# A written order for the loads, norms and projections that open the first layer

## The chip, the cores and the metric

The kernel runs on one core of one Trainium2 chip. The metric is the device time of one execution in microseconds (us). The kernel before takes 2577.58 us, the median of 3 runs (2576.38 to 2580.35). A core has five engines that run side by side, each taking its instructions in the order in which they were laid down: PE (TensorE, the matrix products), DVE (VectorE), ACT (ScalarE), POOL (GpSimd) and SP (SyncE, which here issues almost all DMAs).

## The reference, cut to what matters

Four layers in a row on 1024 tokens of width 1024: two of a first block (with 256 context tokens beside them), two of a second. Only the first layer is touched. It is:

```python
h_l = rmsnorm(x, norm_g[l]) * (1 + sc_l[:, None]) + sh_l[:, None]
h_c = rmsnorm(ctx, norm_g[l]) * (1 + sc_c) + sh_c
f_in, f_gate, q_a, kv_a, k_pe, m_gate = split_cols(h_lat @ w_in, EVEN_SPLITS)
kv = (rmsnorm(kv_a, kv_norm) @ w_kvb)
q = (rmsnorm(q_a, q_norm) @ w_qb)
y_l = concatenate([fourier_mix(f_in) * silu(f_gate), a_l * silu(m_gate)]) @ w_out
```

`sh`, `sc` (shift and scale) are products of `silu(c)` with `w_mod`. `k_pe` and a part of `q` are rotated by the rope tables before the attention `a_l`.

## The kernel before, in words

All activations are kept transposed: features on the 128 partitions, tokens along the row. Tokens come in three chunks, `CH`: c=0 and c=1 are 512 tokens each, c=2 is the context with 256. Every f32 product is made from three matmuls, because activations and weights are split into a high part (rounded) and a low part (the rest): high by high, low by high, high by low. `wblk_steps` (L168) loads a block of weights in pieces into one of two buffers of raw data (`wraw`), ACT makes the high part (L158) and POOL the low part (L166); the split blocks lie in a pool with two slots (`wp`, L103) unless another pool is named.

**Who sets the order.** The program is traced once, and a planner at compile time then lays down each engine's order from priorities (earlier traced goes first if it is ready by the planner's own clock) and allots buffers. `later` (L133) lowers the priority of what is traced in it. `in_order` (L141) takes the instructions that one engine got while the block was traced and fixes their order among themselves; instructions traced outside can still be placed between them. `issue_after` puts instructions behind a given one on its engine.

**`e1_start`** (L505) opens the layer. `START` (L92) is a list of steps: `v` loads the small vectors, `xN` loads chunk N of the input (8 tiles), adds up its squares (ACT squares, DVE adds for c=0 and c=1, POOL for c=2) and then makes its norm (`norm`, L550); with an `a` behind it the norm is left to a step `rN`. A norm is `rstd_bc` (L373): column sums on PE (L358), nine small DVE operations (`rsqrt`, L339), products on PE that spread the result over the partitions (L369), and an ACT copy. `lN` loads a quarter of `w_mod` into four buffers `mraw`, `mN` multiplies it by `silu(c)` (L441, L447) and gives shift and scale for two feature tiles; `wN` loads two of the four pieces of a weight block: w0 is the block of `kv_a`, w1 the first 256 columns of `f_in`. As soon as a quarter q and a chunk c are both there, `modulate(q, c)` writes the two tiles `ah` and `al` of the projections' input on DVE and ACT (L489 to L497). In this block the orders of SP and of DVE are fixed; PE's is the planner's.

**`e1`** (L616) then makes `kv_a` (four tiles for c=0 and c=1) and four blocks of `f_in`, k by k as the inputs arrive; then `kv_a` of the context; then the norm of `kv_a` (`rstd_bc` into `rkt` and `rkb`); then the rest of `f_in` (token blocks j=4 to 9 of the first 256 columns, then all ten of the next 288, the last 32 of which are `k_pe`, copied into `kp` by DVE, L670 and L671); then `kp` is transposed on PE (L679), rotated on DVE and stored; then the key and value projections. `k_evac` (L692) scales each key tile by `rkb`. `mod_rest` (L455) is traced under `later`: 32 loads of 512 KB and 56 DVE passes over them (L474) that make the shifts and scales of later use. The query part follows: `q_a` (by `proj`, L233, with weight blocks of 256 and 128 columns), its squares added up by POOL in `accq` (L389), its norm, and the product with `w_qb`, whose evacuation (L724) needs the norm. Last, `fill` (L746) yields the gate tiles (the SiLU branches), eight steps of three matmuls to a tile: some are laid down under `later`, until `PRE1` = 48 times 512 columns are reached (L782), the others are spread through the attention, whose PE order is written out (`attention`, L267).

Of the kernel before, what the change touches and what calls it, by code (L numbers as in the profile page):

```python
# [15 lines left out]
ALU = mybir.AluOpType  # L16
# [4 lines left out]
P = 128  # L21
T = 1024
TC = 256
TT = T + TC
EPS = 1e-6
MLA_SCALE = float(1.0 / np.sqrt(96.0))
CH = ((0, 512), (512, 1024), (1024, 1280))
# [15 lines left out]
class Kern:  # L43
# [47 lines left out]
    PRE1 = 48  # L91
    START = "v x0a l0 w0 r0 m0 w0 x1 x2 w1 m1 w1 m2 m3"  # L92
    WAYS = "xxxxdddd xxxxdddd xxxxxxxx".split()
# [27 lines left out]
    def stg(self, n=512):  # L121
        return self.t(self.gp_, [P, 512], tag="stg", bufs=4)[:, 0:n]
# [382 lines left out]
    def e1_start(self):  # L505
        V = self.nc.vector
# [27 lines left out]
        act, M, acc = Act(), {}, {}  # L534
# [21 lines left out]
        H, N = set(), []  # L556
        with self.in_order(mybir.EngineType.SP), self.in_order(mybir.EngineType.DVE):
            for what in self.START.split():
                i = int(what[1:2] or 0)
# [56 lines left out]
    def e1(self):  # L616
# [7 lines left out]
        act = self.e1_start()  # L624
        w_in, w_out = A["e_w_in"], A["e_w_out"]
        ALLC = (0, 2, 1)
        mv = self.open("modv", side="left")
        with self.later():
            self.mod_rest(mv)
# [22 lines left out]
        for j, o in enumerate(us):  # L652
            t = stg()
            nc.scalar.activation(out=t, in_=o, func=AF.Copy)
            self.dma(u_scr[j * 256:(j + 1) * 256, 0:256].rearrange("(e p) n -> p e n", p=P), t.rearrange("p (e n) -> p e n", e=2))
        self.proj(wk, ((0, P, 0), (P, P, 1)), act, (2,), ev)
        rkt = self.t(kvp, [P, 10], nm="rkt")
        rkb = self.t(kvp, [P, TT], nm="rkb")
        self.rstd_bc(rkb, acc, TT, 256.0, rkt)
        kp = self.t(kvp, [P, 10, 64], nm="kp")  # L660
        for b, n in ((0, 256), (1, 288)):
            w = self.wblk(w_in, b * 256, n, pool=kvp) if b else wu
            for j in (0, 1, 2, 3, 8, 9, 4, 5, 6, 7) if b else (4, 5, 6, 7, 8, 9):
                s = self.sps()[:, 0:n]
                self.dense_tok(s, w, 0, n, act, j)
                o = stg(256)
                nc.scalar.activation(out=o, in_=s[:, 0:256], func=AF.Copy)
                self.dma(u_scr[j * P:(j + 1) * P, b * 256:(b + 1) * 256], o)
                if b:
                    V.tensor_copy(kp[:, j, 0:32], s[:, 256:288])  # L670
                    V.tensor_copy(kp[:, j, 32:64].rearrange("p (a b) -> p a b", a=2), s[:, 256:288].rearrange("p (a b) -> p a b", a=2)[:, ::-1, :])  # L671
        for c, (a, b) in enumerate(CH):
            tab = self.t(kvp, [32, 2, 512], tag="kpe_tab", bufs=1)
            if c < 2:
                self.dma(tab, A["kpe_tab"][:, :, a:b])
            for e in range(2 if c < 2 else 1):
                s = self.sps()
                for j in range(a // P, b // P):
                    nc.tensor.transpose(s[0:32, j * P - a:j * P - a + P], kp[:, j, 32 * e:32 * e + 32], self.ident)  # L679
                if c == 2:  # L680
                    V.tensor_copy(kpe[:, a:b], s[0:32, 0:b - a])
                elif e == 0:
                    V.tensor_tensor(kpe[:, a:b], s[0:32], tab[:, 0], ALU.mult)
                else:
                    o = stg()[0:32]
                    V.tensor_tensor(o, s[0:32], tab[:, 1], ALU.mult)
                    V.tensor_tensor(kpe[:, a:b], kpe[:, a:b], o, ALU.add)
        self.dma(kpe_scr, kpe)
        w_kvb, w_qb = A["e_w_kvb"], A["e_w_qb"]
        w = self.wblk(w_kvb, 0, 512)  # L690

        def k_evac(i, c, ps):  # L692
# [3 lines left out]
            self.dma(k_scr[i * P:(i + 1) * P, a:b], o)  # L696
        self.proj(w, [(i * P, P, i) for i in range(4)], KV, ALLC, k_evac)
        w = self.wblk(w_kvb, 512, 512)
# [13 lines left out]
        Q = Act(3)  # L712
        ev = self.normed_split(qp, "q", Q, gq, acc, sm)
        w = self.wblk(w_in, 1056, 256)
        self.proj(w, ((0, P, 0), (P, P, 1)), act, ALLC, ev)
        w = self.wblk(w_in, 1312, 128)
        self.proj(w, ((0, P, 2),), act, ALLC, ev)
        rqb = acc
        self.rstd_bc(rqb, acc, TT, 384.0)

# [19 lines left out]
        gate, mix, todo = self.gate_evac(gate_scr, None, gs, 2), Act(), []  # L740

        def gates(w, i, c):
            for e in (0, 1):
                yield from self.dense_steps(w, e * P, act, c, self.FT, lambda ps: gate(i + e, c, ps))

        def fill():  # L746

            for i, c0 in ((0, 544), (2, 800)):
                w = self.wblk(w_in, c0, 256)
                for c in ALLC:  # L750
                    yield from gates(w, i, c)
            W = [(self.wblk(w_in, c0, 256), i) for i, c0 in ((4, 1696), (6, 1952))]
            for c in ALLC:
                for w, i in W:
                    yield from gates(w, i, c)
                todo.extend((k, c) for k in range(8))

# [21 lines left out]
        am_scr = dram("am_scr", [512, TT])  # L779
        f, before = fill(), 0  # L780
        with self.later():
# [1381 lines left out]
```

## Time and profile before

| | us |
|---|---|
| median of 3 runs | 2577.58 |
| lowest, highest | 2576.38, 2580.35 |
| the profiled execution | 2578.05 |
| its span (first to last instruction) | 2576.2 |
| PE busy | 2428.7 (94%) |
| DVE, ACT, POOL busy | 1681.6, 1126.9, 895.3 |
| mean granted TensorE clock | 0.976 of full speed |

A row of a wait gives the total, how often, and the longest. A row of a window gives its length, the busy time of PE, of PE's weight loads, of DVE, ACT and POOL (instructions in brackets), then the granted clock, the share of the DMA engines that was busy, and GB/s. A row in order of time gives start, length, engine, line, operation, what is written from what, the sizes, and how many instructions are merged.

All times in the rows are counted from the start of the span. An engine's idle time stands in square brackets behind the instruction that ended it, with what was waited for. Matmuls overlap in the records, so the pace is read from start to start. The granted clock is given as a share of full speed: 1.00 is 2.4 GHz, 0.50 is 1.2 GHz, and a figure between is a mix of the two over the stretch.

### The profile page before, as it was taken

To read this page: it belongs to the slowest core of one execution; us is meant where nothing else is said; L and a number is where in the kernel's file an instruction comes from. 1 tells how busy PE (TensorE), PEld (TensorE's weight loads), DVE (VectorE), ACT (ScalarE), POOL (GpSimd) and SP (SyncE) were. 2 spreads that over 40 slices of the span, in tenths; PEclk is the share of its full clock that TensorE was granted. 3 is DMA by queue.
4 is the path that set the end of the run, shared out by engine and by line. 5 is a ranking of instruction groups with operands and counts; after the bars stand their busy time and mean duration, and the time that the engine had idled before them with its cause. 6 is when DMAs were issued, how large, how long until landed. Compare 5 with 4: busy or idle time off the path is not lost. (4 is left out here: it accounts for less than half of the span.)

```text
span 2576.2 us, 36051 instructions
## 1 busy us (share of the span) xinstructions
PE 2428.7 (94%) x12814; PEld 1962.3 (76%) x12814; DVE 1681.6 (65%) x2983; ACT 1126.9 (44%) x2201; POOL 895.3 (35%) x750
## 2 busy tenths in 40 slices
PE   5999999999999989999898999999999999999998
PEld 3887777777678877666666779887877877799888
DVE  6785447788855548777776463557888576773455
ACT  4412226666653325655565333345656333513331
POOL 4204243354411152332322225146452343453231
PEclk7999999999999999999999999999999999999999
DMA  7475432132324231221313513233233332201433
GB/s 240 137 223 197 155 105 57 47 102 76 96 82 146 84 90 52 67 87 52 101 64 111 164 66 97 90 108 98 85 105 122 101 114 79 70 21 49 165 111 103
DMA packets 217092, 265.16 MB, mean 103 GB/s; under 512 B 42768, under 2 KB 142768, under 8 KB 216784
## 3 DMA queue, kind: packets, MB, share of 16 engines
q1 hardware_dynamic: 216192, 262.75, 32.7%
q8 instruction: 101, 1.65, 0.3%
q14 instruction: 79, 0.65, 0.1%
q10 hardware_dynamic: 720, 0.10, 0.0%
HBM read 188.60 MB, written 71.97 MB: 101 GB/s over the span
## 5 line engine op out<-in xcount | busy, mean ns | idle before, releaser
L166 POOL TENSOR_TENSOR wlo<-wraw,whi 128x512 fp32r<-128x512 f32 (+3 forms) x229 | 318.3, 1401 | 608.3 <-ACT whi L158 531.4
L166 DVE TENSOR_TENSOR pl<-pf,ph 128x512 fp32r<-128x512 f32 (+1 forms) x328 | 258.6, 789 | 79.1 <-ACT pf L953 39.8
L158 ACT ACTIVATE whi<-wraw 128x512 fp32r<-128x512 f32 (+3 forms) x261 | 154.3, 613 | 341.5 <-PE s L209 53.2
L209 PE MATMUL s<-ah,whi 128*128 128x512 f32 (+1 forms) x392 | 159.3, 406 | 12.2 <-DVE hf L1725 5.9
L209 PE MATMUL s<-al,whi 128*128 128x512 f32 (+1 forms) x392 | 158.0, 403 | 1.8 <-DVE al L492 1.4
L209 PE MATMUL s<-ah,wlo 128*128 128x512 f32 (+1 forms) x392 | 157.4, 402 | 0.0
L953 ACT ACTIVATE ph<-s 128x512 fp32r<-128x512 f32 (+1 forms) x176 | 101.5, 577 | 105.8 <-PE s L950 104.9
L915 DVE TENSOR_REDUCE mx<-p 128x1 f32<-128x512 f32 (+1 forms) x208 | 116.7, 574 | 34.5 <-PE p L914 33.5
L1250 ACT ACTIVATE ph<-s 128x512 fp32r<-128x512 f32 x152 | 90.8, 597 | 108.7 <-PE s L1242 58.4
L209 PE MATMUL g<-ah,whi 128*128 128x512 f32 (+1 forms) x312 | 122.5, 393 | 3.3 <-DVE mixg L382 3.3
L209 PE MATMUL f<-ah,whi 128*128 128x512 f32 x304 | 123.2, 405 | 1.3 <-DVE stg L1361 0.8
L209 PE MATMUL f<-ah,wlo 128*128 128x512 f32 x304 | 122.8, 404 | 0.0
L209 PE MATMUL f<-al,whi 128*128 128x512 f32 x304 | 122.8, 404 | 0.0
L209 PE MATMUL g<-ah,wlo 128*128 128x512 f32 (+1 forms) x312 | 121.7, 390 | 0.0
L209 PE MATMUL g<-al,whi 128*128 128x512 f32 (+1 forms) x312 | 121.5, 390 | 0.0
L1614 DVE TENSOR_TENSOR_SCAN scu<-scu,ones_col 128x128 f32<-128x128 f32 (+3 forms) x64 | 97.4, 1535 | 14.4 <-ACT scu L1610 11.6
L1210 DVE CUSTOM_DVE_ANT_0 p<-p,maskt 128x384 f32<-128x384 f32 (+1 forms) x128 | 67.4, 529 | 58.1 <-PE p L1209 58.1
L953 ACT ACTIVATE pf<-s 128x512 f32<-128x512 f32 (+1 forms) x176 | 100.8, 573 | 2.0 <-DVE pl L166 1.9
L209 PEld LDWEIGHTS s<-ah,whi 128*128 128x128 f32 x392 | 75.3, 192 | 34.2 <-DVE hf L1725 6.8
L474 DVE CUSTOM_DVE_ANT_0 wmj<-wmt,srow,c_b_mod 128x1024 bf16<-128x1024 f32 x56 | 77.0, 1376 | 29.0 <-DMA wmt<-in_w_modT 28.0
L209 PEld LDWEIGHTS s<-al,whi 128*128 128x128 f32 x392 | 75.4, 192 | 20.6 <-DVE al L492 2.1
L1250 ACT ACTIVATE pf<-s 128x512 f32<-128x512 f32 x152 | 90.1, 593 | 0.1
(775 smaller groups left out, 7568.9 us busy)
## 6 DMA issues: line engine op xcount, KB each, us to landing
wmt<-in_w_modT SPq DMA_DIRECT2D x32, 512.0 KB
wraw<-in_even_w_in SPq DMA_DIRECT2D x56, 256.0 KB
wraw<-in_odd_w_in SPq DMA_DIRECT2D x48, 256.0 KB
wraw<-in_o_w_in SPq DMA_DIRECT2D x40, 256.0 KB
xold<-x_scr SPq DMA_DIRECT2D x40, 256.0 KB
mraw<-in_w_mod SPq DMA_DIRECT2D x16, 512.0 KB
x_scr<-x SPq DMA_DIRECT2D x32, 256.0 KB
mixx<-m_scr SPq DMA_DIRECT2D x30, 256.0 KB
```

The source lines that it names most:

```text
L158: nc.scalar.activation(out=out, in_=in_, func=AF.Copy)
L166: return e.tensor_tensor(out, in_, hi.bitcast(F32), ALU.subtract)
L209: self.nc.tensor.matmul(out, ws[:, k, c:c + m], a[k][ch], start=first and i == j == 0, stop=last and i == len(ks) - 1 and j == 2)
L474: V.tensor_tensor_reduce(out=junk, in0=w, in1=s[:, i], scale=0.5, scalar=self.bm[l][:, m, i:i + 1], op0=ALU.mult, op1=ALU.add, accum_out=s ...
L915: V.reduce_max(mx[:, e, j:j + 1], d[:, 0:y - x], axis=AX)
L953: nc.scalar.activation(out=t, in_=s, func=AF.Exp, scale=MLA_SCALE)
L1210: V.tensor_tensor_reduce(out=d[:, 0:n], in0=d[:, 0:n], in1=self.mask[:, off:off + n], scale=1.0, scalar=-3.0e38, op0=ALU.add, op1=ALU.max, ...
L1250: nc.scalar.activation(out=t, in_=s, func=AF.Exp, scale=0.125)
L1614: V.tensor_tensor_scan(out=rev, data0=rev, data1=self.ones.to_broadcast([P, n]), initial=1.0, op0=ALU.mult, op1=ALU.mult)
```

## The change

Four parts. (1) `START` is put into another order, and PE's order in this block is fixed too. The second chunk's load is split from its norm, the second quarter of `w_mod` is loaded and multiplied before that norm, and the context comes last. `mod_rest` is put behind the start's DMAs. (2) After the start PE's order is fixed as: `f_in` j=8, 9; `kv_a` of the context; j=4, 5; the sums of the norm; j=6, 7; the spreading of the norm; then the 288 columns. (3) The transposes of `kp` become a generator of five turns, of which two are taken after each chunk of the key projection, in a fixed PE order. (4) In the query part two gate tiles of c=0 (16 steps of `fill`) stand between the projection and its norm, in a fixed PE order; the 128-column weights move to the query part's own pool `qp`; the steps count towards `PRE1`. The cut diff:

```diff
-    START = "v x0a l0 w0 r0 m0 w0 x1 x2 w1 m1 w1 m2 m3"
+    START = "v x0a l0 r0 w0 m0 x1a w1 l1 m1 r1 w0 w1 l2 m2 l3 m3 x2"
...
-        with self.in_order(mybir.EngineType.SP), self.in_order(mybir.EngineType.DVE):
+        with self.in_order(mybir.EngineType.SP), self.in_order(mybir.EngineType.DVE), self.in_order():
...
-        with self.later():
+        with self.later(), self.tc.issue_after(self.first_dmas):
             self.mod_rest(mv)
...
-        self.proj(wk, ((0, P, 0), (P, P, 1)), act, (2,), ev)
...
-        self.rstd_bc(rkb, acc, TT, 256.0, rkt)
...
-        for b, n in ((0, 256), (1, 288)):
-            w = self.wblk(w_in, b * 256, n, pool=kvp) if b else wu
-            for j in (0, 1, 2, 3, 8, 9, 4, 5, 6, 7) if b else (4, 5, 6, 7, 8, 9):
+        def u_proj(w, b, n, js):
+            for j in js:
...
+        with self.in_order():
+            u_proj(wu, 0, 256, (8, 9))
+            self.proj(wk, ((0, P, 0), (P, P, 1)), act, (2,), ev)
+            u_proj(wu, 0, 256, (4, 5))
+            self.rstd_cols(acc, TT // P, 256.0, rkt)
+            u_proj(wu, 0, 256, (6, 7))
+            self.bcast_cols(rkt, TT // P, rkb)
+            u_proj(self.wblk(w_in, 256, 288, pool=kvp), 1, 288, (0, 1, 2, 3, 8, 9, 4, 5, 6, 7))
...
+        turns = rotate_kpe()
...
-        self.proj(w, [(i * P, P, i) for i in range(4)], KV, ALLC, k_evac)
+        with self.in_order():
+            for c in ALLC:
+                self.proj(w, [(i * P, P, i) for i in range(4)], KV, (c,), k_evac)
+                next(turns)
+                next(turns, None)
+            for _ in turns:
+                pass
...
+        gate = self.gate_evac(gate_scr)
...
+        f, before = fill(), 0
         w = self.wblk(w_in, 1056, 256)
-        self.proj(w, ((0, P, 0), (P, P, 1)), act, ALLC, ev)
-        w = self.wblk(w_in, 1312, 128)
-        self.proj(w, ((0, P, 2),), act, ALLC, ev)
+        w2 = self.wblk(w_in, 1312, 128, pool=qp)
         rqb = acc
-        self.rstd_bc(rqb, acc, TT, 384.0)
+        with self.in_order():
+            self.proj(w, ((0, P, 0), (P, P, 1)), act, ALLC, ev)
+            self.proj(w2, ((0, P, 2),), act, ALLC, ev)
+            for _ in range(16):
+                before += next(f)
+            self.rstd_bc(rqb, acc, TT, 384.0)
...
-        f, before = fill(), 0
         with self.later():
             while before < self.PRE1 * 512:
                 before += next(f)
```

`rotate_kpe` holds the old loop over `CH` with a `yield` after each transposed group, and `gates` and `fill` are moved up unchanged.

## Rows read from the trace of the kernel before

**Rows 1.** Page, busy time of PE.
```profile
PE 2428.7 (94%) x12814; PEld 1962.3 (76%) x12814; DVE 1681.6 (65%) x2983; ACT 1126.9 (44%) x2201; POOL 895.3 (35%) x750
```

**Rows 2.** PE in order of time, first layer up to the 288 columns.
```profile
28.73 0.79 PE L209 MATMUL s<-ah,whi 128*128 128x512 f32 x1 [3.23 <-ACT ah L490]
...
97.65 0.28 PE L221 MATMUL g<-whi,ach 128*128 128x256 f32 x1
...
107.59 0.36 PE L221 MATMUL o<-whi,ah 128*128 128x256 f32 x1
...
110.51 0.28 PE L221 MATMUL p<-whi,ah 128*128 128x256 f32 x1
...
123.42 0.29 PE L221 MATMUL s<-whi,ah 128*128 128x288 f32 x1
```

**Rows 3.** Windows of 20 us in the start.
```profile
40.00:60.00 20.00, 17.07 (x80) 9.82 (x84) 14.88 (x20) 5.73 (x12) 15.07 (x13) 0.75 0.50 162
...
60.00:80.00 20.00, 18.78 (x90) 12.05 (x83) 14.69 (x36) 8.57 (x17) 0.00 (x0) 0.83 0.38 123
```

**Rows 4.** DVE in order of time, in the start.
```profile
32.88 5.45 DVE L389 TENSOR_TENSOR acc<-acc,sq 128x512 f32<-128x512 f32 x7
...
48.02 3.55 DVE L489 SCALAR_TENSOR_TENSOR mh_t<-x,mc,rb 128x512 f32<-128x512 f32 x2 [2.86 <-ACT rb L371]
...
65.47 0.75 DVE L489 SCALAR_TENSOR_TENSOR mh_t<-x,mc,rb 128x512 f32<-128x512 f32 x1
...
77.03 0.55 DVE L495 TENSOR_SCALAR mh_t<-x,mc,ms 128x512 f32<-128x512 f32 x1
...
77.49 0.68 DVE L166 TENSOR_TENSOR al<-mh_t,ah 128x512 fp32r<-128x512 f32 x1
...
89.19 0.49 DVE L492 SCALAR_TENSOR_TENSOR acl<-mh_t,ms,ach 128x256 fp32r<-128x256 f32 x1 [0.18 <-ACT ach L490]
```

**Rows 5.** SP's DMA issues in the start, in order of time.
```profile
25.00 4.92 SPq L128 DMA_DIRECT2D x<-in_ctxT  x7
...
32.91 1.96 SPq L128 DMA_DIRECT2D mraw<-in_w_mod  x4
...
89.74 0.73 SPq L128 DMA_DIRECT2D kpe_tab<-in_kpe_tab  x1
```

**Rows 6.** DMA traffic in 40 slices of the first 100 us.
```profile
GB/s 60 297 296 256 377 403 240 2 132 323 325 376 339 231 321 352 117 123 309 0 51 278 264 155 256 356 349 20 0 0 7 0 0 0 0 0 115 283 358 168
```

**Rows 7.** DVE in order of time: the norm of `kv_a` and two passes.
```profile
116.60 0.16 DVE L360 TENSOR_SCALAR rs_s<-f 128x10 f32<-128x10 f32 x1
...
126.44 2.39 DVE L474 CUSTOM_DVE_ANT_0 wmj<-wmt,srow,c_b_mod 128x1024 bf16<-128x1024 f32 x1
...
131.41 0.17 DVE L351 SCALAR_TENSOR_TENSOR rkt<-rs_t,rkt 128x10 f32<-128x10 f32 x1
...
196.69 1.29 DVE L474 CUSTOM_DVE_ANT_0 wmj<-wmt,srow,c_b_mod 128x1024 bf16<-128x1024 f32 x1 [3.87 <-DMA wmt<-in_w_modT]
```

**Rows 8.** PE's waits from 94 to 400 us.
```profile
PE f L358 <- POOL accq L389: 4.6, 1, 4.6
...
PE f L369 <- DVE rkt L351: 3.1, 1, 3.1
...
PE g L679 <- DVE kp L670: 1.9, 1, 1.9
...
PE p L209 <- DVE kpe L683: 1.4, 1, 1.4
```

**Rows 9.** Windows behind two of these waits.
```profile
131.70:135.70 4.00, 3.97 (x19) 4.00 (x20) 2.78 (x7) 0.60 (x1) 0.00 (x0) 0.57 0.90 268
...
243.70:251.70 8.00, 7.96 (x26) 6.80 (x27) 8.00 (x9) 1.87 (x5) 6.17 (x6) 0.51 0.12 33
```

**Rows 10.** PE in order of time, ahead of the attention.
```profile
330.53 0.58 PE L209 MATMUL g<-ah,whi 128*128 128x512 f32 x1
...
352.91 0.40 PE L914 MATMUL p<-kh,qh 96*128 96x512 f32 x1
```

More of the change, by code (lines that the diff above doesn't have):

```diff
@@ L671, in e1 @@
                     V.tensor_copy(kp[:, j, 32:64].rearrange("p (a b) -> p a b", a=2), s[:, 256:288].rearrange("p (a b) -> p a b", a=2)[:, ::-1, :])
[L672 to L687, printed above, removed]
@@ L688, in e1, with rotate_kpe @@
-        self.dma(kpe_scr, kpe)
+        def rotate_kpe():
+            for c, (a, b) in enumerate(CH):
+                tab = self.t(kvp, [32, 2, 512], tag="kpe_tab", bufs=1)
+                if c < 2:
+                    self.dma(tab, A["kpe_tab"][:, :, a:b])
+                for e in range(2 if c < 2 else 1):
+                    s = self.sps()
+                    for j in range(a // P, b // P):
+                        nc.tensor.transpose(s[0:32, j * P - a:j * P - a + P], kp[:, j, 32 * e:32 * e + 32], self.ident)
+                    if c == 2:
+                        V.tensor_copy(kpe[:, a:b], s[0:32, 0:b - a])
+                    elif e == 0:
+                        V.tensor_tensor(kpe[:, a:b], s[0:32], tab[:, 0], ALU.mult)
+                    else:
+                        o = stg()[0:32]
+                        V.tensor_tensor(o, s[0:32], tab[:, 1], ALU.mult)
+                        V.tensor_tensor(kpe[:, a:b], kpe[:, a:b], o, ALU.add)
+                    yield
+            self.dma(kpe_scr, kpe)
@@ L713, in e1, with gates, fill @@
         ev = self.normed_split(qp, "q", Q, gq, acc, sm)
+        gate = self.gate_evac(gate_scr)
+        def gates(w, i, c):
+            for e in (0, 1):
+                yield from self.dense_steps(w, e * P, act, c, self.FT, lambda ps: gate(i + e, c, ps))
+        def fill():
+            for i, c0 in ((0, 544), (2, 800)):
+                w = self.wblk(w_in, c0, 256)
+                for c in ALLC:
+                    yield from gates(w, i, c)
+            W = [(self.wblk(w_in, c0, 256), i) for i, c0 in ((4, 1696), (6, 1952))]
+            for c in ALLC:
+                for w, i in W:
+                    yield from gates(w, i, c)
+                todo.extend((k, c) for k in range(8))
+        f, before = fill(), 0
         w = self.wblk(w_in, 1056, 256)
-        self.proj(w, ((0, P, 0), (P, P, 1)), act, ALLC, ev)
-        w = self.wblk(w_in, 1312, 128)
-        self.proj(w, ((0, P, 2),), act, ALLC, ev)
+        w2 = self.wblk(w_in, 1312, 128, pool=qp)
         rqb = acc
-        self.rstd_bc(rqb, acc, TT, 384.0)
+        with self.in_order():
[4 more added lines that the diff above has]
+            self.rstd_bc(rqb, acc, TT, 384.0)
         def q_evac(i, c, ps):
@@ L740, in e1 @@
         gate, mix, todo = self.gate_evac(gate_scr, None, gs, 2), Act(), []
[L742 to L756, printed above, removed]
         def add():
```

## The prediction, as it was made before the run

> **What bounds the kernel now.** I read the page's busy times first: PE is busy for 94% of the span [rows 1]. So time is to be had where PE stands still or runs at the lower clock, and I looked for these places in the stretch that the change touches, which ends with the first product of the attention at 352.9 us [rows 10]. The order of time on PE shows a first projection at 28.73 us and the last of that batch ending at 97.65, where block j=8 begins [rows 2]. The work between is about 48 us at full clock: 34.2 for the projections (four blocks of 24 products at 0.244 us and four at 0.122, twice and once the pace of 256 columns in rows 2: 110.51 - 107.59 = 2.92 us for 24), some 14 for shifts, scales and norms. 69 us passed. The windows say why: a granted clock of 0.75 and 0.83 of full speed [rows 3], PE being fed piece by piece.
>
> What feeds it is DVE, whose order is fixed. The order of time on DVE [rows 4]: the second chunk's squares are added until 38.3 us, its norm lets the first modulation of that chunk begin at 48.0, the context's last tile is written at 89.2, and only then does SP get past its release and issue the next loads at 89.74 [rows 5]. Call that moment E. The second quarter of `w_mod` is issued at 32.91, behind the context [rows 5], and the traffic has holes from 32.5 us on although 7 MB are still to come [rows 6]. After the start the list of PE's waits [rows 8] has four that matter: 4.6 us for the squares of `q_a` on POOL, 3.1 for the norm of `kv_a`, 1.9 and 1.4 around the transposes of `kp`. The windows behind the first two run at 0.51 and 0.57 of full clock [rows 9].
>
> **The change part by part.** Sums are made against the profiled execution, 2578.05 us (span 2576.2 and 1.85 around it), which lies 0.47 above the median.
>
> **The start.** Nothing is added or left out; 16 `mraw`, 24 input and 8 weight DMAs change places on SP, and PE's shifts, scales and norms are put in line. Until the second chunk's sums (38.3 us) DVE's order is the same. Then: `m1` 0.5; quarter 1 of c=0, four operations, which take 0.75 us where POOL rests and 3.55 / 2 = 1.78 where it works [rows 4], so 3.0 to 7.1, I take 4.5; the norm, 9.7 in the trace (38.3 to 48.0) with POOL at work and perhaps 9.7 x 0.75 / 1.78 = 4.1 without, I take 7; four tiles of c=1, 6.0 to 14.2, I take 10; `m2` 0.5 and four tiles of 0.55 + 0.68 [rows 4], 4.9; the same again for `m3`, 5.4 in all; the context's norm 5; its eight tiles at 2 x 0.49, 7.8. E = 38.3 + 0.5 + 4.5 + 7 + 10 + 5.4 + 5.4 + 5 + 7.8 = 83.9. With POOL at rest throughout it is 74.6. POOL is busy 15.1 us between 40 and 60 and not at all from 60 to 80 [rows 3], and DVE can lose no more to it than POOL works, so 90 is the other end. The loads don't set E: 15.7 MB at the 300 GB/s that the better slices show [rows 6] are in by 54 us, and with the buffers handed back late (the third quarter behind the norm's spreading on PE, some 51 us, then 2.1 MB and 1 MB at that rate) by 64; the context's sums are wanted at 71.
>
> From E to the 288 columns PE had 123.4 - 89.2 = 34.2 us of work left. Now the first batch is done by about E, as 46 us of work have 55 us to run in, and there remain the end of j=8 (0.4), j=9 (2.9), `kv_a` of the context (5.8), j=4 to 7 (11.6), the sums (2.4), and 2 us that I add for a low clock while j=8 follows the context's tiles one by one: 25.1. So the 288 columns are reached at 109.0 in place of 123.4: **14.4 us** gained. If PE gets no denser than it was (48 in 69 us), 46 us of work take 66, the batch ends at 95, and only 3 are gained; with E at 74.6 and no low clock 25. I take the sum as worked out, as E's row-by-row value lies between its ends.
>
> A row shows the same instruction at 1.78 and at 0.75 us. The Trainium skill (SBUF — State Buffer, SBUF: two separate sides) says why: an operation of DVE with two SBUF inputs and one of GpSimd take the same port pair as an exclusive lock and the other fully blocks. It speaks against this change, as nothing takes work off POOL. By that rule every us of POOL's work could hold up DVE, E would be 90 and the sum 6 us poorer; by the rows of 60 to 80 us, where POOL rests, it is 83.9.
>
> **The norm of `kv_a`.** Before, the spreading stood where the planner thought the norm ready, and PE waited 3.1 us and lost 4.0 x (1 - 0.57) = 1.7 to the clock [rows 8, 9]. Now it stands behind j=6 and 7, 5.8 us after the sums, and the 288 columns are queued behind it on PE. The norm's nine small operations went from 116.60 to 131.58, 15.0 us, since the planner put a pass of `mod_rest` between every two [rows 7]; DVE's order is not fixed here, so I expect that again. 9.2 us stay open. The key products of c=0 (24 at 0.244, 5.9 us) are outside the block and may be put in; I count half, and 1 us of clock: 7 in place of 4.8, a **loss of 2.2**. Ends: all covered, a gain of 4.8; and if each step waits for a pass of 2.39 and half of a load's 3.87 [rows 7], 9 x 4.3 - 5.8 = 33 us open, a loss of 28.
>
> The Trainium skill (TensorE: Matmul & The Clock Gate, Step-by-step: what each phase is for) has matmuls stay in program order. Rows 8 agree: 3.1 us passed with later products ready. By that rule nothing but an order laid down beforehand fills the 9.2 us.
>
> **The transposes.** 1.9 + 1.4 = 3.3 us of waits [rows 8]; between the turns there are now four key tiles (5.9 or 2.9 us), longer than either wait. DVE is nearly full there with `mod_rest`, so I take **3**; ends 0 and 3.3.
>
> **The query part.** The 4.6 us for POOL's last square and the low clock behind it, 8.0 x (1 - 0.51) = 3.9 [rows 8, 9], make 8.5. Two gate tiles of 24 products of 512 columns (11.7 us) now cover it. Their four weight loads come before `w_qb` on SP and through ACT and POOL, their results take two of four staging buffers, and their block keeps one of two slots until its later tiles are done, so that the last `w_qb` block waits for the one before it. I take **7**; ends 0 (the gate's weights are late, SP standing behind `mod_rest`) and 8.5.
>
> **Ahead of the attention.** From 330.53 to 352.91 us [rows 10] PE worked on gate tiles while keys and queries were fetched and split. One tile of 512 columns (5.9) is gone from there, as the count to `PRE1` includes the two. I take a **loss of 2**; ends 0 and 8 (the tile and 2 of clock).
>
> Sum: 14.4 - 2.2 + 3 + 7 - 2 = 20.2; 2578.05 - 20.2 = 2557.9, and 2557.4 on the median's scale. I say 2558.
>
> **The rivals.**
> *PE gets no denser* (start gains 3, not 14.4): 2569. For it: feeding stays piecewise, POOL's work is unchanged. Against it: four load-to-product latencies are pulled ahead of two norms.
> *The order is only on paper.* The fixed order binds shifts and norms among themselves, the projections stay the planner's, and SP still waits for the same buffers; the start is unchanged and 5.8 are left: 2572. For it: SP's order was fixed before as well. Against it: quarter 1 now stands ahead of the context's load.
> *The norm of `kv_a` holds PE* (slower). It sits at the spreading in the 288 columns' queue, with the price of 33 us worked out above; it decides from 27 us on, where it eats 14.4 + 3 + 7 - 2 + 4.8. Time: 2578 - 22.4 - 4.8 + 33 = 2584. For it: nine steps between passes; against it: it took 15.0, not 39.
> *Better*: E at 74.6 and the norm covered: 14.4 + 9 + 4.8 + 3 + 7 - 2 = 36, 2542.
>
> **How the numbers follow.** Forecast 0.60 (its own range 2547 to 2569), no denser 0.17, on paper 0.06, the norm holds PE 0.08, better 0.09. From 2543 to 2575 some 0.8 are in. 0.2% (5.2 us) is about what a measurement can tell here. Faster by more: 0.60 + 0.13 + 0.09 + 0.02 = 0.84; slower: 0.08 and 0.01 from accidents; within: 0.07.
>
> **What would show it.** The context's last tile at 84 us on DVE; the 288 columns begun at about 109 on PE, later by what the spreading waits; a wait for `rkt` of 3 to 9 us; no wait for `accq`, `kp`, `kpe`; the first product of the attention near 333. Wrong it is if the 288 columns begin after 118, or if a new wait of over 10 us appears.

## The result and the profile after

The changed kernel is slower: 2597.54 us, the median of 6 runs (2590.47 to 2602.05), against 2578.58 for the kernel before (6 runs, 2576.18 to 2583.72). The ratio is 1.0068 with a 95% interval of 1.0055 to 1.0082: some 17 us by the ratio, 19 by the two medians. The prediction said 2558 (2543 to 2575) and has the wrong sign. The profiled execution took 2594.35 us, its span is 2592.6.

PE did the same work (2425.4 us busy, 94%, against [rows 1]); it stood still at other places. PE in order of time, the changed kernel, up to the 288 columns (it answers to [rows 2]; lines behind the changed part of `e1` stand up to 20 higher than before):

```profile
28.50 0.80 PE L209 MATMUL s<-ah,whi 128*128 128x512 f32 x1
...
88.53 0.28 PE L221 MATMUL p<-whi,al 128*128 128x256 f32 x1
100.33 0.58 PE L221 MATMUL s<-whi,ach 128*128 128x256 f32 x1 [11.53 <-ACT acck L386]
...
123.97 0.37 PE L358 MATMUL f<-ones_col,acck 128*128 128x1 f32 x1 [3.41 <-POOL acck L389]
...
139.57 2.05 PE L369 MATMUL f<-c_ident,rkt 128*128 128x128 f32 x8 [6.21 <-DVE rkt L351]
142.30 2.07 PE L369 MATMUL f<-c_ident,rkt 128*128 128x128 f32 x8 [0.69 <-ACT rkb L371]
...
145.93 0.59 PE L221 MATMUL s<-whi,ah 128*128 128x288 f32 x1
...
179.95 0.30 PE L221 MATMUL p<-whi,al 128*128 128x288 f32 x1
```

The last product of the 288 columns in the kernel before:

```profile
162.18 0.29 PE L221 MATMUL p<-whi,al 128*128 128x288 f32 x1
```

The first batch ends at 88.8, 9 us earlier than before. Then j=8, the first of the new order, is next and PE stands still for 11.5 us; what it waits for is the square of a `kv_a` tile (L386), an evacuation of the PSUM buffer `s` that j=8 is to write. (PSUM buffers take the products that PE writes; ACT and DVE read them out, here called evacuation, before a buffer is written anew.) After that the sums wait 3.4 us for the context's squares and the spreading 6.2 us for the norm. The 288 columns begin at 145.93 where they began at 123.42. (Part of that is order: before, the spreading stood between the 288 columns, so their end is the fairer mark: the last product begins at 179.95 against 162.18, 17.8 us later.)

DVE in order of time, in the start (it answers to [rows 4]), says when the inputs came:

```profile
46.30 0.16 DVE L351 SCALAR_TENSOR_TENSOR rs_r<-rs_t,rs_r 128x4 f32<-128x4 f32 x1
53.24 3.54 DVE L489 SCALAR_TENSOR_TENSOR mh_t<-x,mc,rb 128x512 f32<-128x512 f32 x2 [6.79 <-ACT rb L371]
...
75.20 0.16 DVE L451 TENSOR_TENSOR ms<-f,c_b_mod 128x4 f32<-128x4 f32 x1 [1.89 <-PE f L447]
...
82.39 0.16 DVE L351 SCALAR_TENSOR_TENSOR rs_r<-rs_t,rs_r 128x2 f32<-128x2 f32 x1
88.43 0.88 DVE L489 SCALAR_TENSOR_TENSOR mh_t<-x,mc,rb 128x256 f32<-128x256 f32 x2 [5.88 <-ACT rb L371]
...
95.66 0.49 DVE L492 SCALAR_TENSOR_TENSOR acl<-mh_t,ms,ach 128x256 fp32r<-128x256 f32 x1 [0.18 <-ACT ach L490]
96.95 0.75 DVE L598 SCALAR_TENSOR_TENSOR kvl<-s,c_e_kv_norm,kvh 128x512 fp32r<-128x512 f32 x1 [0.80 <-ACT kvh L597]
```

The context's last tile ends at 96.15, not at the predicted 83.9 and later than before (89.68). The nine steps of both norms took 1.7 us each (the last ones stand at 46.30 and 82.39), and then DVE stood idle for 6.8 and 5.9 us until the spreading on PE was done. And the last row shows why j=8 stood: the first evacuation of `kv_a`, whose products ended at 88.8, comes only after the context's tiles. ACT in order of time, the changed kernel, has the same, up to the square that frees buffer `s`:

```profile
95.11 0.51 ACT L490 ACTIVATE ach<-mh_t,ms 128x256 fp32r<-128x256 f32 x1 [0.41 <-DVE mh_t L489]
96.23 0.69 ACT L597 ACTIVATE kvh<-s,c_e_kv_norm 128x512 fp32r<-128x512 f32 x1 [0.60 <-DVE acl L492]
...
99.67 0.61 ACT L386 ACTIVATE acck<-s 128x512 f32<-128x512 f32 x1
```

Windows of 20 us of the changed kernel (they answer to [rows 3, 9]; columns as there):

```profile
40.00:60.00 20.00, 15.23 (x84) 12.04 (x84) 12.51 (x20) 4.42 (x7) 8.35 (x6) 0.80 0.59 205
60.00:80.00 20.00, 20.00 (x97) 12.71 (x96) 14.96 (x31) 9.43 (x20) 5.72 (x7) 0.94 0.26 77
80.00:100.00 20.00, 8.80 (x52) 7.55 (x50) 12.03 (x31) 8.29 (x17) 0.65 (x1) 0.83 0.10 26
120.00:140.00 20.00, 10.39 (x60) 10.13 (x60) 17.91 (x33) 2.74 (x7) 4.42 (x4) 0.77 0.63 199
140.00:160.00 20.00, 18.63 (x109) 18.04 (x109) 16.03 (x31) 2.73 (x6) 0.00 (x0) 0.72 0.59 191
```

From 60 to 80 PE is denser than before, as was meant (20.0 us at 0.94 against 18.78 at 0.83); from 80 to 100 it works 8.8 us, from 120 to 140 10.4, and behind the second stretch the granted clock is 0.72.

PE's waits from 80 to 400 us (they answer to [rows 8]):

```profile
PE s L221 <- ACT acck L386: 11.5, 1, 11.5
PE p L934 <- POOL qh L160: 7.3, 1, 7.3
PE f L369 <- DVE rkt L351: 6.2, 1, 6.2
PE f L358 <- POOL acck L389: 3.4, 1, 3.4
```

The waits for `accq`, `kp` and `kpe` are gone, as predicted. A new one of 7.3 us stands ahead of the attention's first product (`qh`, the split queries). That product begins at 372.24 against 352.91 [rows 10], 19.3 us later, and the span ends 16.4 us later: what is lost is lost by here. (20 products of the moved gate tiles now stand ahead of it, some 5 us of the 19.3 at the prediction's 0.244 us each.)

### The profile page after: what moved, and what is told of

It is laid out like the page before. It is cut to its first block, busy times and chain, and to the rows that moved or that the text cites. A ratio compares the mean times of both kernels' runs of the same rounds, so it can differ in the third digit from the quotient of the medians.

```text
span 2592.6 us, 36044 instructions
## 1 busy us (share of the span) xinstructions
PE 2425.4 (94%) x12814; PEld 1958.4 (76%) x12814; DVE 1684.2 (65%) x2983; ACT 1127.1 (43%) x2201; POOL 889.8 (34%) x750
## 5 line engine op out<-in xcount | busy, mean ns | idle before, releaser
L166 DVE TENSOR_TENSOR pl<-pf,ph 128x512 fp32r<-128x512 f32 (+1 forms) x328 | 253.1, 772 | 81.3 <-ACT pf L973 41.2
L209 PE MATMUL p<-ah,wlo 128*128 128x512 f32 x224 | 89.0, 401 | 1.0 <-POOL wlo L166 1.0
```

Source lines behind the costliest of these rows:

```text
L166: return e.tensor_tensor(out, in_, hi.bitcast(F32), ALU.subtract)
L209: self.nc.tensor.matmul(out, ws[:, k, c:c + m], a[k][ch], start=first and i == j == 0, stop=last and i == len(ks) - 1 and j == 2)
```

## The experiments

Eighteen runs, in five groups, each compared with runs of the kernel before beside it (medians 2572.4 to 2575.9 us there). Ratios, not times, are compared between groups; differences under 0.15% say nothing. The traces are single executions, which lie up to 7 us off their kernel's median. The table has all runs; three marks are read from each trace: the first of the 288 columns (PE), the issue of the fetch `u` for the Fourier part (SP), and the attention's first product (PE). The last mark compares like with like only among kernels that have as many gate products ahead of it: with the gate tiles of part 4 there are 20 more than before (68 more in e8), in e11 and e14 7 fewer.

| run | ratio to before (95%) | 288 columns | fetch of `u` | attention |
|---|---|---|---|---|
| before, again (e9) | 1.0007 (0.9994 to 1.0020) | 123.41 | 226.65 | 352.89 |
| changed kernel | 1.0068 (1.0055 to 1.0082) | 145.93 | 224.35 | 372.24 |
| e1 old start | 1.0103 (1.0087 to 1.0120) | 145.74 | 219.12 | 377.33 |
| e2 old block | 1.0050 (1.0034 to 1.0067) | 125.16 | 225.10 | 367.28 |
| e3 parts 3 and 4 alone | 1.0048 (1.0031 to 1.0065) | 124.07 | 224.68 | 366.42 |
| e4 PE's start unordered | 1.0084 (1.0062 to 1.0106) | 143.02 | 217.61 | 373.79 |
| e5 no gate tiles | 1.0070 (1.0052 to 1.0088) | 146.10 | 224.48 | 362.85 |
| e6 part 3 alone | 1.0023 (1.0011 to 1.0035) | 122.42 | 225.22 | 357.24 |
| e7 other buffers | 1.0061 (1.0041 to 1.0080) | 139.93 | 226.56 | 371.50 |
| e8 e3, two gate tiles more | 1.0050 (1.0030 to 1.0070) | 124.39 | 226.34 | 377.29 |
| e10 buffers and norm | 1.0005 (0.9994 to 1.0016) | 125.25 | 240.41 | 365.93 |
| e11 e10 without gate tiles | 1.0024 (1.0011 to 1.0037) | 124.21 | 234.81 | 359.27 |
| e12 before, four buffers | 0.9970 (0.9955 to 0.9984) | 124.01 | 204.74 | 340.51 |
| e13 e10, four buffers | 0.9975 (0.9963 to 0.9986) | 126.42 | 221.22 | 355.00 |
| e14 e11, four buffers | 0.9984 (0.9974 to 0.9995) | 122.87 | 213.15 | 350.57 |
| e15 e12 with part 3 | 0.9972 (0.9960 to 0.9983) | 125.14 | 206.63 | 344.76 |
| e16 changed, four buffers | 1.0067 (1.0050 to 1.0084) | 145.18 | 211.22 | 367.97 |
| e17 norm alone | 1.0080 (1.0065 to 1.0095) | 133.72 | 250.57 | 378.47 |
| e18 e12 with the new start | 0.9971 (0.9956 to 0.9986) | 123.94 | 205.63 | 341.53 |

### Which part loses it: e1 to e4

```diff
e1 (changed kernel):
-    START = "v x0a l0 r0 w0 m0 x1a w1 l1 m1 r1 w0 w1 l2 m2 l3 m3 x2"
+    START = "v x0a l0 w0 r0 m0 w0 x1 x2 w1 m1 w1 m2 m3"
-... self.in_order(mybir.EngineType.DVE), self.in_order():
+... self.in_order(mybir.EngineType.DVE):
-        with self.later(), self.tc.issue_after(self.first_dmas):
+        with self.later():
e2 (changed kernel):
-        with self.in_order():
-            u_proj(wu, 0, 256, (8, 9))
-...
+        self.proj(wk, ((0, P, 0), (P, P, 1)), act, (2,), ev)
+        self.rstd_bc(rkb, acc, TT, 256.0, rkt)
+        u_proj(wu, 0, 256, (4, 5, 6, 7, 8, 9))
+        u_proj(self.wblk(w_in, 256, 288, pool=kvp), 1, 288, (0, 1, 2, 3, 8, 9, 4, 5, 6, 7))
e3: both of these. e4 (changed kernel):
-... self.in_order(mybir.EngineType.DVE), self.in_order():
+... self.in_order(mybir.EngineType.DVE):
```

> The changed kernel with its new start undone (old order of loads and norms, PE's shifts and norms not put in line, the rest of the modulation not held back); block order, spread transposes and gate tiles as changed. Theory A (the order of the block behind the first batch loses the time: j=8 stands first, takes a PSUM buffer that a projection of kv_a still holds, and the sums' norm waits behind it): the wait ahead of j=8 stays over 5 us, the 288 columns begin at 135 to 142, and the time is 2583 to 2592. Rival B (the new start loses it, by a context that is loaded last): all comes back, the 288 columns begin by 123 and the time is 2560 to 2572.

> The changed kernel with the block's order undone: kv_a of the context, sums and spreading together, then j=4 to 9, all at the planner's choice as in the kernel before; new start, spread transposes and gate tiles kept. Theory A (the block's order loses it): products of j=4 to 7 fill the 11.5 us in which PE stood still, the 288 columns begin at 119 to 124, and the time is 2570 to 2577. Rival B (the new start loses it): the context's products still wait for a last tile at 96, the 288 columns begin at 130 or later, and the time is 2583 or more.

> The kernel before with only the two later parts of the change: the keys' transposes spread over the key products, and two gate tiles between the query projection and its norm. By the traces the lag against the kernel before went from 17.8 us at the 288 columns to 16.4 at the end of the span, so theory A gives 1.4 us gained, 2574 to 2579. The prediction's own terms (3 + 7 - 2) would give 8 gained, 2570. Rival C (the gate tiles lose time, since the 7.3 us wait ahead of the attention takes the place of the cover that they were): 2582 or more.

> The changed kernel with one thing undone: PE's shifts, scales and norms of the start are no longer put in line, the planner places them. Theory A (the spreadings stand late because the projections are laid ahead of them, which the line among norms doesn't touch): the context's last tile stays between 94 and 98 us, the wait ahead of j=8 stays at about 11 us, and the time is 2592 to 2600. Rival D (the line itself delays the modulations): the context's last tile comes back to 90 or earlier, and the time is 2590 or less.

With the old start the new block is still slower (e1, 1.0103, 26 us where theory A said 5 to 14), so rival B falls. Against e3, which differs by the block only, the block costs 0.55% or 14 us. But theory A had the wrong wait: in e1 the batch's last product begins at 98.97 and j=8 at 99.34, with hardly a wait between, and yet the 288 columns begin at 145.74, as in the changed kernel. PE waits 2.5 us for the sums there and 9.0 for the spreading:

```profile
139.37 2.05 PE L369 MATMUL f<-c_ident,rkt 128*128 128x128 f32 x8 [9.05 <-DVE rkt L351]
```

So the wait ahead of j=8 in the changed kernel uses up what the new start had gained there, and the rest is lost behind it. With the old block (e2) the 288 columns are back at 125.16, but the kernel is as slow as e3: beside the old block the new start gains nothing. That e3 itself is 0.48% slower was expected by rival C alone. In e4 the context's last tile comes at 91.1, between theory A's 94 to 98 and rival D's 90, so the line among PE's norms does hold back the modulations, as rival D said; yet j=8 still waits 8.5 us and the time does not come back, as theory A said.

### Two waits of the block: e7, e17, e10

```diff
e7 (changed kernel; u_proj hands tags to sps):
-            u_proj(wu, 0, 256, (8, 9))
+            u_proj(wu, 0, 256, (8, 9), "gf")
e17 (changed kernel):
-        with self.later(), self.tc.issue_after(self.first_dmas):
-            self.mod_rest(mv)
...
             self.rstd_cols(acc, TT // P, 256.0, rkt)
+            norm = next(i for i in reversed(nc.cur_bb.bb.instructions) if i.engine == mybir.EngineType.DVE)
+            with self.later(), self.tc.issue_after(self.first_dmas), self.tc.issue_after(norm):
+                self.mod_rest(mv)
e10: both
```

> The changed kernel with one thing changed: j=8 and j=9 take the PSUM buffers g and f, which are free then, in place of s, which a projection of kv_a holds until its evacuation. Theory P (the buffer is what held j=8 for 11.5 us): j=8 begins with the context's tiles, by 91 us, and is done by 98, the 288 columns begin 5 to 8 us earlier than in the changed kernel; of that a part is lost again in later slack, 14 to 18 us above the kernel before. Rival Q (the context's tiles hold it): j=8 begins by 91 too but ends no earlier than 101, and the 288 columns come within 2 us of the changed kernel's 145.9.

> The changed kernel with the passes of the second half of the modulation queued behind the norm of kv_a, and the PSUM buffers as changed. Theory N (the norm is what holds the block; j=8's buffer costs only where nothing later waits longer): the wait for rkt is below 2 us, the wait of 11.5 ahead of j=8 stays, the 288 columns begin at 130 to 135, and the time is 3 to 9 us above the kernel before. Rival M (the two add, each with half): 9 to 13 us above the kernel before.

> The changed kernel with both of its new waits in the block taken away: j=8 and j=9 use the PSUM buffers g and f, and the passes of the second half of the modulation are queued on DVE behind the norm of kv_a, so that they can't stand between its nine steps. Theory P (buffer and norm hold the block): the wait for rkt falls from 13.3 us (with the buffers alone) below 3, and the 288 columns begin at 122 to 127 in place of 145.9. Theory S (what PE gains before 200 us is lost again by 300, because the fetches for the Fourier part and the queries' weights follow the modulation's stream of loads, which ends near 225 us in every trace): the time is no lower than with the old block (14 us above the kernel before). Rival T (PE's order alone paces it): 15 to 20 us below the changed kernel, 0 to 4 above the kernel before.

PE in order of time with other buffers (e7): j=9 takes buffer `f` at 96.56, 3.8 us before the changed kernel begins j=8. That is theory P: the buffer held j=8, not the context's data. (The buffer's share is less than the 11.5 us, as j=8 now begins at 89.65 and follows the context's tiles one by one; j=9 comes 8.0 us earlier, 96.56 against 104.61.) But the gain runs into the next wait:

```profile
96.56 0.28 PE L221 MATMUL f<-whi,ach 128*128 128x256 f32 x1
...
133.56 0.77 PE L369 MATMUL f<-c_ident,rkt 128*128 128x128 f32 x2 [13.27 <-DVE rkt L351]
...
139.93 0.59 PE L221 MATMUL g<-whi,ah 128*128 128x288 f32 x1
```

The norm's nine steps now take from 118.65 to 133.42 on DVE, because a pass of `mod_rest` stands between every two, and the spreading waits 13.3 us. Queued ahead of the passes (e10) the same nine steps take 1.8 us. DVE in order of time, then PE:

```profile
115.14 0.17 DVE L360 TENSOR_SCALAR rs_s<-f 128x10 f32<-128x10 f32 x1 [6.05 <-PE f L358]
...
116.78 0.17 DVE L351 SCALAR_TENSOR_TENSOR rkt<-rs_t,rkt 128x10 f32<-128x10 f32 x1
```

```profile
120.72 1.05 PE L369 MATMUL f<-c_ident,rkt 128*128 128x128 f32 x8
122.94 1.16 PE L369 MATMUL f<-c_ident,rkt 128*128 128x128 f32 x8 [1.17 <-ACT rkb L371]
...
125.25 0.38 PE L221 MATMUL g<-whi,ah 128*128 128x288 f32 x1
```

With both waits gone the 288 columns begin at 125.25 (P: 122 to 127) and the kernel is level with the kernel before, by the ratios 0.63% or 16 us faster than the changed one; theory S, which expected 14 us above, falls here, and rival T's range holds it. So mending the two waits together takes the loss away. It is not shown that they are the only loss: the parts don't add, as the two later parts alone cost 0.48% beside the old block (e3), and e10 has them and is level. Nor do the two waits add: each mended alone gives nothing that can be told from noise (e7 1.0061, e17 1.0080, the latter against both of its theories). e17 ends the 288 columns 13 us earlier than the changed kernel (the last product at 166.54) and issues the fetch of `u` 26 us later. The passes, put behind a norm that is itself late, end at 250.5, and the sums of the query norm then wait 11.5 us (see the next section).

The Trainium skill (Perfetto Trace Analysis, Matmuls) has independent groups rotate through different PSUM banks, so that one's evacuation overlaps the next one's products. The 11.5 us and what e7 does to them agree.

### A second path to the attention: e12

The fetch of `u` follows the last pass of `mod_rest` in all 20 traces, in 14 of them within 0.1 us, as its tiles take room that the pool `modv` gives back. DVE's last pass and SP's fetch, in the kernel before:

```profile
225.01 1.56 DVE L474 CUSTOM_DVE_ANT_0 wmj<-wmt,srow,c_b_mod 128x1024 bf16<-128x1024 f32 x1 [1.27 <-DMA wmt<-in_w_modT]
```

```profile
226.61 4.87 SPq L128 DMA_DIRECT2D u<-u_scr  x10
```

The pass ends at 226.57, the fetch is issued at 226.61. From there to the attention's first product there are 126.3 us before, 126.2 in e9, 125.5 in e10, 124.5 in e11, 127.9 in e17, and more in all others; never less. The trace of the kernel before shows where this path meets PE. POOL in order of time, then PE:

```profile
235.78 1.68 POOL L806 TENSOR_TENSOR u<-fa,fa 128x512 f32<-128x512 f32 x1 [6.55 <-DMA u<-u_scr]
...
241.97 2.85 POOL L389 TENSOR_TENSOR accq<-accq,stg 128x512 f32<-128x512 f32 x2
```

```profile
243.74 1.87 PE L358 MATMUL f<-ones_col,accq 128*128 128x1 f32 x8 [4.56 <-POOL accq L389]
```

POOL's additions of the Fourier part stand idle 6.55 us for the fetched tiles, `q_a`'s squares are queued behind them, and the sums of the query norm on PE wait 4.56 us for these. In e10 PE is 5.2 us ahead of the kernel before at the end of the 288 columns (the last product at 156.94), the fetch comes 14 us later, and the same sums wait 9.8 us, for a gate tile's evacuation that DVE has among the Fourier part's additions:

```profile
254.75 4.40 PE L358 MATMUL f<-ones_col,accq 128*128 128x1 f32 x20 [9.84 <-DVE stg L382]
```

If that is a path of its own, a shorter stream must bring the attention forward:

```diff
e12 (kernel before):
-        t = self.t(mp, [P, 1024], tag="wmt", bufs=2)
+        t = self.t(mp, [P, 1024], tag="wmt", bufs=4)
-                w = self.t(mp, [P, 1024], tag="wmt", bufs=2)
+                w = self.t(mp, [P, 1024], tag="wmt", bufs=4)
-        rkb = self.t(kvp, [P, TT], nm="rkb")
+        rkb = acc
```

> The kernel before, unchanged, as a yardstick: its trace on the chip of the other experiments, and what two sets of runs of one kernel differ by. Every theory expects the ratio to hold 1.000 in its interval of about 0.15% to either side; an interval that lies off 1 by more would make the differences of 0.2 to 0.7% of the other runs doubtful.

> The kernel before with four buffers in place of two for the rows of w_modT (room for them by letting the spread norm of kv_a take the place of its sums). Theory S (this stream of loads paces 160 to 300 us): its last pass on DVE ends 15 us or more ahead of 225, the Fourier part's fetches are issued earlier by as much, and the time is 4 to 12 us below the kernel before. Rival T (PE's order alone paces it): within 3 us of the kernel before.

With four buffers the stream ends 22 us earlier (DVE, SP and PE of e12):

```profile
203.42 1.28 DVE L474 CUSTOM_DVE_ANT_0 wmj<-wmt,srow,c_b_mod 128x1024 bf16<-128x1024 f32 x1 [0.97 <-DMA wmt<-in_w_modT]
```

```profile
204.74 5.20 SPq L128 DMA_DIRECT2D u<-u_scr  x10
```

```profile
340.51 0.39 PE L914 MATMUL p<-kh,qh 96*128 96x512 f32 x1
```

The attention begins 12.4 us earlier (135.8 us behind the fetch, so that now something else ends last), and the time is 0.30% lower, about 8 us: with e15 and e18, which hold the same edit, the fastest of all, and faster than both kernels of the case. PE has the same work ahead of the attention as in the kernel before. Not all of the 12.4 us come from behind the fetch. The query projection begins 6.8 us earlier, ahead of either fetch; the kernel before, then e12:

```profile
195.61 0.39 PE L209 MATMUL p<-ah,whi 128*128 128x512 f32 x1
```

```profile
188.83 0.39 PE L209 MATMUL p<-ah,whi 128*128 128x512 f32 x1
...
233.61 1.05 PE L358 MATMUL f<-ones_col,accq 128*128 128x1 f32 x8 [1.22 <-POOL accq L389]
```

PE waits 1.0 us for `rkt` there and none for `kp` and `kpe`, against 3.1, 1.9 and 1.4 before. The other 5.6 us are gained by the end of the query norm, whose sums wait 2.0 us in all in place of 4.6, and behind which the 8 us from 233.6 run at a granted clock of 1.00, where the kernel before had 0.51 behind them [rows 9]. The edit also lets `rkb` take the place of `acc`, and no run parts that from the buffers. So before the change PE did wait at this norm behind the stream; how much of a gain on PE's own path it would have hidden is not shown by a run of its own.

### The later parts, and the start alone

```diff
e6 (kernel before): part 3 alone. e15: e12 with part 3. e18: e12 with part 1.
e5 (changed kernel), e11 (e10):
-        w2 = self.wblk(w_in, 1312, 128, pool=qp)
...
-            for _ in range(16):
-                before += next(f)
+        w = self.wblk(w_in, 1312, 128)
e13, e14, e16: e10, e11 and the changed kernel with the edit of e12
e8 (e3): PRE1 = 64, and
-        with self.later():
-            while before < self.PRE1 * 512:
-                before += next(f)
         with self.in_order():
+            with self.later():
+                while before < self.PRE1 * 512:
+                    before += next(f)
             self.mla(kq, ...
```

> The changed kernel without its last part: no gate tiles between the query projections and their norm, which is taken at once, as before. Theory G (the gate tiles ahead of the norm put off the queries by their own length and are missing as cover ahead of the attention, which costs 13 to 16 us between 300 and 372 us): the wait for the split queries ahead of the attention's first product falls below 2 us, the wait for POOL's last square at the query norm comes back with 3 to 5 us, and the time is 2 to 8 us above the kernel before. Rival A (all the loss is in the block behind the first batch): 17 us or more above the kernel before.

> The kernel before with one part of the change alone: the keys' transposes spread over the key products. By the two traces it gains about 2 us, by the prediction 3: 1 to 4 us below the kernel before. Rival: this part is what cost the 14 us of the run with the two later parts, 5 us or more above the kernel before; no wait of the trace names it.

> The kernel before with the two later parts of the change, and with two gate tiles more, laid ahead of the attention's first product (8 in place of 6 before the attention). Theory G (the loss of these parts is cover missing ahead of the attention): the wait for the split queries, 8.7 us without these tiles, falls below 2 us, and the time is 2 to 6 us above the kernel before, where it was 14 without them. Rival H (the attention begins later by as much as the tiles take, or lacks them later): 10 us or more above the kernel before.

> The same, and the gate tiles between the query projections and their norm undone as well; what is left of the change is the start, the block with both waits mended, and the spread transposes. Theory G (the gate tiles are taken from the cover ahead of the attention): the wait for the split queries is below 2 us, and the time is 6 to 12 us below the run with the gate tiles, 2 to 8 above the kernel before. Rival: the same time as with the gate tiles, within 3 us.

> The changed kernel with both waits of the block mended (buffers g and f for j=8 and 9, the modulation's passes behind the norm), and four buffers for the rows of w_modT. Theory S (the stream took what PE gained): its last pass ends by 220, the queries' stretch no longer waits, and the time is 10 to 16 us below the kernel before, at or a little below the kernel before with four buffers alone (9 below). Rival G (the gate tiles are taken from the cover ahead of the attention, whatever the stream does): the wait for the split queries stays over 5 us and the time is 0 to 6 below the kernel before.

> The same without the gate tiles between the query projections and their norm. Theory S with G: no wait for the split queries, and 3 to 8 us below the run with the gate tiles. Rival (the gate tiles fill idle time that is there anyway): 2 us or more above it.

> The kernel before with four buffers and the spread transposes. Theory S (these lost 5 us in the kernel before because they put off what stands behind the stream of w_modT rows): within 3 us of the kernel before with four buffers alone, that is 6 to 12 us below the kernel before. Rival (spread transposes cost by themselves, as their multiplications queue between the keys' on a DVE that is full): 3 to 6 us below the kernel before.

> The changed kernel with four buffers for the rows of w_modT and nothing else. Theory P (the two waits of the block cost by themselves, before the stream matters): the wait ahead of j=8 stays near 11 us, and the time is 5 to 13 us above the kernel before. Rival S alone (the stream is what turns the block's delay into lost time): 0 to 9 us below the kernel before.

> The kernel before with four buffers for the rows of w_modT and the new start alone: loads, norms and PE's shifts in the written order, the modulation's second half behind its last load; block, transposes and query part as before. The prediction's term (14.4 us) would give 20 to 25 us below the kernel before. Theory E (the first batch ends 9 us earlier, but the context's last tile, loaded last, comes 6.5 us later, and kv_a's sums wait for it): the batch ends by 90, the context's last tile is at 95 to 97, the 288 columns begin no earlier than 121, and the time is 6 to 12 us below the kernel before, as with four buffers alone.

**Gate tiles.** Theory G is wrong as stated. Without them the wait ahead of the attention is gone (e5, e11, e14) and its first product comes 4 to 9 us earlier, but the two tiles (11.7 us of PE) are then still to be done: e5 is level with the changed kernel, e11 0.19% above e10, e14 0.09% above e13, while in the kernel before they cost 0.25% (e3 against e6). Two tiles more ahead of the attention (e8) take its wait away and give nothing either; a wait of 6.4 us for the Fourier part's tables stands there instead. They are cover that is moved, not gained.

**Spread transposes.** Alone 0.23% slower (e6, some 6 us), against the expectation and in the rival's range; with four buffers e15 equals e12. They gain nothing in either; why they cost in the first is not settled. The wait for `accq` is longer there (7.9 us in its list of PE's waits, against 4.6 and 5.3 in the two traces of before).

**The start.** e18 is level with e12 (0.9971, 0.9970), with the stream out of the way: there was no gain to be taken. Its batch ends at 87.4 and the context's last tile at 94.7, close to what theory E said, and `kv_a` of the context then waits 3.5 us for a PSUM buffer. The 288 columns begin where they did.

**The changed kernel with four buffers** (e16) stays 0.67% slower, above theory P's range and far from rival S: its loss is not the stream's. With both waits mended as well (e13) it is 0.25% faster than the kernel before, between its two theories, and no better than e12.

## Why the prediction was wrong

Both signs that the prediction named for being wrong came: the 288 columns began after 118, and a new wait of over 10 us appeared.

**The start: 14.4 us gained; measured nothing.** Two steps of this term failed. The first is E = 83.9; it was 96.15, 12.2 us later. By the prediction's own sum the second chunk's norm should have been spread at 50.3 and its tiles begun; they began at 53.24 [6.79 idle]. `m3` should have followed `m2` at about 66; it came at 75.20, waiting for its products on PE (the quarter begun by `m2` at 63.06 took 12.1 us, not 5.4). The context's norm was given 5 us and took 7.6, from 80.82 to 88.43, of which 1.7 were its steps. "PE's shifts, scales and norms are put in line" was taken to bring the norms forward, but products were laid ahead of the spreadings, as before; the line binds them only among themselves. Ranked last in the order, the context took the whole delay.

The second failed step is "From E to the 288 columns PE had ... 25.1 us of work left", summed as if PE could take it up as soon as the inputs were there. It asked which inputs j=8 needs and not which PSUM buffer; the buffer was the later of the two (100.3 against 96.2). The first batch did end early (88.8 against 97.8), PE being denser from 60 to 80, as argued; then it had no buffer to write to. From the start of j=8 to the 288 columns it took 45.6 us in place of 25.1: the waits of 3.4 and 6.2 us, 6.4 us of the spreading, which now stands ahead of them, and a low clock (0.77 from 120 to 140). e1, in which j=8 hardly waits, reaches the 288 columns no sooner. (Of the sums ahead of these steps one does not come out: with the paces stated, 0.244 and 0.122 us, the projections are 35.1 us and not 34.2. Nothing rests on the difference.)

**The norm of `kv_a`: a loss of 2.2, with an end of 28.** The mechanism was named (a pass between every two steps), its size was about right (the nine steps took 11.2 us, 128.26 to 139.43, in place of 15.0), and 6.2 us of the 9.2 left open showed up as a wait. What was missed is the wait of 3.4 us ahead of the sums, where `kv_a`'s evacuations stand between passes too. e10 shows the price of the passes: 1.8 us without them.

**The transposes: 3 gained.** The waits for `kp` and `kpe` went. The gain is not to be found in e6 or e15.

**The query part: 7, and ahead of the attention: -2.** The wait for `accq` went too, with its low clock. The second term was mis-sized: two of the six tiles counted by `PRE1` moved out of the cover, and the wait for `qh` (7.3 us) came. Together the runs put the two between a gain of 5 and a loss of 6 us, in place of 5 gained.

**The rivals.** None had it. The slower one put the price at the spreading alone, and let it decide from 27 us open; what came was 11.5 us at the PSUM buffer, 3.4 at the sums, 6.2 at the spreading and the low clock behind them. "The order is only on paper" was right on the norms' spreading, and wrong in that nothing would be lost by it.

**The rule on ports.** The Trainium skill (SBUF — State Buffer, SBUF: two separate sides) would have had E at 90, by POOL's work blocking DVE. No run here shows a lock by itself: the same operation again takes 1.77 us (3.54 for two at 53.24), but what made E late were DVE's idle stretches, not slow operations.

**A question that the prediction did not ask** is whether PE's path to the attention is the longest at all. In the kernel before it was not: PE waited at the query norm behind the stream of `w_modT` rows, and what e10 had gained by the 288 columns (5.2 us) was waited out there (9.8 us). So a part of the forecast 20.2 us could not have shown even if the start had gained it; how large a part is not measured.

## What to carry to other kernels

An order written out for PE is only as good as the order of the engines that hand back its PSUM buffers: for each step of a new order ask for the buffer as well as for the inputs, and see whether its evacuation is laid behind other work. Nine dependent small operations cost 1.8 us in a row and 11 to 15 when a background job may step in between. Before pricing waits on the busiest engine, look for a second path to the same point, here a stream of loads with two buffers whose memory the next stage needs: e12, with two buffers more, gave what the whole change did not.

## What had not been expected

The distance from the fetch of `u` to the attention was within 124.5 and 127.9 us in five traces whose 288 columns begin up to 10 us apart, so a background stream can set the pace of a stage in which PE is over 90% busy (163.3 of the 172.9 us from 180 us to the attention, in the kernel before). And a wait costs more than its length: the windows with and behind the waits of 11.5, 3.4 and 6.2 us (80 to 100, 120 to 140, 140 to 160) were granted 0.83, 0.77 and 0.72 of full speed, where the kernel before was granted 1.00, 0.91 and 1.00:

```profile
80.00:100.00 20.00, 20.00 (x124) 17.85 (x124) 13.42 (x25) 11.38 (x20) 3.82 (x3) 1.00 0.36 116
...
120.00:140.00 20.00, 16.87 (x122) 16.67 (x121) 15.70 (x30) 4.15 (x10) 3.04 (x2) 0.91 0.70 211
140.00:160.00 20.00, 20.00 (x154) 20.00 (x153) 16.82 (x35) 2.98 (x8) 0.00 (x0) 1.00 0.64 186
```
